# Seven block products for eight in the down projection and the embedding's gate of a decoder trunk

## The chip, the cores and the metric

The kernel runs on one core of a Trainium2 chip. The metric is the device time of one execution in microseconds (us). The engines are TensorE (PE in the profile; its weight loads are PEld), VectorE (DVE), ScalarE (ACT), GpSimd (POOL) and SyncE (SP), which issues the loads of the weights. They run side by side and wait for each other on semaphores.

## The reference

Two layers over 256 tokens of width 2048, all in fp32. In each layer the stream h receives three additions:

```
h += Mixer(RMSNorm(h))                                  # latent attention in layer 0, gated delta rule in layer 1
gate, up = split(RMSNorm(h) @ w_gate_up)                # 2048 x (2 x 5632)
h += (silu(gate) * up) @ w_down                         # 5632 x 2048
h += RMSNorm(p[i] @ w_proj) * sigmoid(RMSNorm(h) @ w_gate)   # w_gate 2048 x 2048
```

The mixers, which the change does not touch beyond their buffers, have projections of the same kind.

## The kernel before

**Products.** A weight is loaded in tiles of 4 k-tiles by 512 columns (`wload`, line 99; a tile `raw`, 1 MB). `wsplit` (L104) makes of it a rounded part `wh` (a cast on ScalarE, L109) and the remainder `wl` (a subtraction on VectorE, L110). The activations are split likewise, into `xh` and `xl`, after TensorE has transposed them (`make_xT`, L146). One product of a k-tile is then three matmuls of 512 columns, `xh wh`, `xh wl`, `xl wh` (`products`, L312 to L316). The 256 tokens are two row halves, t = 0 and 1. `linear` (L294) takes one block of 512 columns at a time: two banks of PSUM, one for each t, and for each k-tile two products, six matmuls. When a block is done its `evac` reads the banks.

**Seven for eight.** In the gate/up projection `seven` (L318) takes a gate block (columns c1) and an up block (c2) together. The first 8 of the 16 k-tiles form a 2 by 2 block matrix on both sides: A11 to A22 are the two token halves by the two groups of four k-tiles, b11 to b22 the two groups by the two blocks. Instead of eight block products it makes seven, of sums of blocks: A11 b11, S1 (b12 - b11), A12 b21, S2, S4 b22, S3, and A22. The sums of weight blocks are built on VectorE (L346, L356, L363, L372), those of activations once per norm (`Norm.operands`, L206). Four banks A, C, B, D take the results; two are copied in between by ScalarE (B from A, L351; m5, L353; u2, L360), and D begins as an addition on VectorE (L367). A call of one product over the four k-tiles is a `phase`: 12 matmuls. The other 8 k-tiles follow in the plain form, in phases of 12 as well.

**Stages.** `ffn` (L620) works in four parts of 3, 3, 3 and 2 middle blocks of 512: the part's gate/up calls, then the down projection of these blocks into all of h, with `linear`. Ahead of the last down projection `embed` (L649) makes the embedding's projection. `ple` (L682) is the gate, with `linear`. As soon as a block of h is complete, `Norm.block` (L258) makes the next stage's operands of it.

**What sets the order.** Each engine runs its instructions in one fixed order. The framework that builds the program fixes it: it takes the instructions in the order of the text as long as, by its own estimate, what they need is ready, and otherwise lets later ones pass. `tick` (L270) and `later` (L276) put small work (transposes of a finished block) between matmuls, a set number of ticks later.

**Buffers.** `raw`, `wh` and `wl` have three buffers each in a pool of the whole kernel (`WBUFS`, L40), and in `ffn` two, one and one more (`EXTRA`, L41; `wtile`, L90), so four for split weights there and three elsewhere. `S4` (L39) is the number of shared tiles of 128 x 1024, `P2` (L47) that of the 128 x 512 tiles of each stage. PSUM has four banks for products and four for transposes.

## Time and profile before

| | us |
|---|---|
| median of 3 runs (2805.26 to 2807.74) | 2806.23 |
| the profiled execution, its own time | 2807.84 |
| its span, first to last instruction | 2805.8 |
| PE matmuls busy (99%) | 2774.5 |
| VectorE busy (69%) | 1946.2 |
| ScalarE busy (51%) | 1443.5 |

A matmul's record is longer than its share of the engine, since matmuls are pipelined: the distance from one to the next is the cost. In lists by group, the number behind the last bar is the time that the engine sat idle just before such instructions, and what ended it. The gate/up and down projections of layer 0 run from about 297 to 1021 us, the embedding's projection inside it from 959 to 970, the gate from 1021 to 1089; layer 1 has the same stages from about 1990 to the end.

### The profile page before, as it was taken

The page shows a single profiled execution, that of the slowest core. Times are in us where ns is not written, and L with a number is a line of the kernel's source. Part 1 is how long each engine was busy: PE and PEld are TensorE (multiplying, and loading weights), DVE is VectorE, ACT ScalarE, POOL GpSimd, SP SyncE. Part 2 cuts the span into 40 slices and gives each one's busy share as a digit, 9 for nine tenths or more (in the row PEclk, how much of TensorE's full clock was granted, in tenths as well). Part 3 has the DMA queues.
Part 4 walks back from the last instruction along what each step waited for, and adds up shares of the span by engine and source line. Part 5 has one row for each costly group of instructions (what it writes and reads, how often), then busy time and mean ns, then how long its engine had stood idle before and what let it go on. Part 6 is the DMA issues. An engine that isn't in the chain of part 4 may idle for free.

```text
span 2805.8 us, 33510 instructions
## 1 busy us (share of the span) xinstructions
PE 2774.5 (99%) x13609; PEld 2300.1 (82%) x13609; DVE 1946.2 (69%) x1818; ACT 1443.5 (51%) x1517; POOL 161.6 (6%) x254
## 2 busy tenths in 40 slices
PE   8999999999999999999999999999999999999999
PEld 8778888888888888788888888888788888888887
DVE  5675876877867765556774556657985876867764
ACT  6765653654544555645444444444663554554553
POOL 1430000000000000222100000000000000000000
PEclk9999999999999999999999999999999999999999
DMA  7435465565565545666777545546555464655554
GB/s 225 128 115 190 165 246 174 210 210 171 189 225 195 196 154 175 210 223 213 268 247 237 189 150 188 174 159 215 180 207 198 173 232 150 240 195 194 183 171 145
DMA packets 296444, 540.81 MB, mean 193 GB/s; under 512 B 34105, under 2 KB 55266, under 8 KB 296034
## 3 DMA queue, kind: packets, MB, share of 16 engines
q1 hardware_dynamic: 295858, 536.58, 56.4%
q8 instruction: 107, 1.75, 0.3%
q10 hardware_dynamic: 432, 2.10, 0.2%
q14 instruction: 47, 0.39, 0.0%
HBM read 517.63 MB, written 21.00 MB: 192 GB/s over the span
## 4 chain that ended last, share of the span: by engine, by line
PE 50%; DVE 1%; ACT 1%; issue 1%; DMA 0%; POOL 0%; DVEq 0%; ACTq 0%
PE mm L314 15%; PE mm L316 15%; PE mm L315 15%; PE tr L965 1%; PE tr L1074 1%; PE tr L1080 1%; PE tr L155 1%; DVE wl L110 1%; ACT wh L109 0%; DMA raw<-in_ffn_w_gate_up 0%; PE tr L808 0%; PE tr L868 0%; PE tr L1055 0%; DVE vb L1133 0%; POOL r8o L122 0%
## 5 line engine op out<-in xcount | busy, mean ns | idle before, releaser
L110 DVE TENSOR_TENSOR wl<-raw,wh 128x2048 fp32r<-128x2048 f32 (+4 forms) x514 | 1120.7, 2191 | 546.6 <-ACT wh L109 545.6
L314 PE MATMUL mm<-wh,xh 128*128 128x512 f32 (+1 forms) x3600 | 1414.1, 393 | 5.2 <-ACT wh L109 5.1
L316 PE MATMUL mm<-wh,xl 128*128 128x512 f32 (+1 forms) x3600 | 1395.3, 388 | 0.0
L315 PE MATMUL mm<-wl,xh 128*128 128x512 f32 (+1 forms) x3600 | 1392.1, 387 | 0.9 <-DVE wl L110 0.9
L109 ACT CAST wh<-raw 128x2048 fp32r<-128x2048 f32 (+4 forms) x514 | 936.3, 1826 | 741.3 <-PE mm L316 588.6
L314 PEld LDWEIGHTS mm<-wh,xh 128*128 128x128 f32 x3600 | 678.4, 189 | 141.4 <-ACT wh L109 6.7
L316 PEld LDWEIGHTS mm<-wh,xl 128*128 128x128 f32 x3600 | 677.5, 188 | 138.1 <-DVE xl L593 0.2
L315 PEld LDWEIGHTS mm<-wl,xh 128*128 128x128 f32 x3600 | 678.8, 189 | 131.5 <-DVE wl L110 2.2
L109 ACT CAST wh<-tm 128x2048 fp32r<-128x2048 f32 x44 | 84.0, 1909 | 135.9 <-PE mm L316 115.0
L110 DVE TENSOR_TENSOR wl<-tm,wh 128x2048 fp32r<-128x2048 f32 x44 | 100.6, 2286 | 28.7 <-ACT wh L109 28.6
L400 DVE TENSOR_TENSOR h<-h,mm 128x512 f32<-128x512 f32 x104 | 68.8, 682 | 25.0 <-PE mm L316 24.9
L122 POOL TENSOR_TENSOR re<-re,neghalf 128x2 f32<-128x2 f32 x2 | 5.4, 2704 | 1348.0 <-DVE re L672 1348.0
L631 ACT ACTIVATE sg<-mm,rs 128x512 f32<-128x512 f32 x44 | 30.3, 689 | 62.1 <-PE mm L316 62.1
L346 DVE TENSOR_TENSOR tm<-raw 128x2048 f32<-128x2048 f32 x22 | 50.3, 2288 | 14.0 <-DMA raw<-in_ffn_w_gate_up 14.0
L363 DVE TENSOR_TENSOR raw<-raw 128x2048 f32<-128x2048 f32 x22 | 50.3, 2284 | 1.0 <-DMA raw<-in_ffn_w_gate_up 1.0
L356 DVE TENSOR_TENSOR tm<-raw,tm 128x2048 f32<-128x2048 f32 x22 | 50.4, 2292 | 0.7
L372 DVE TENSOR_TENSOR raw<-raw,tm 128x2048 f32<-128x2048 f32 x22 | 50.3, 2285 | 0.2
L164 ACT ACTIVATE xh<-tr,ncol 128x256 fp32r<-128x256 f32 x88 | 38.9, 476 | 22.2 <-PE tr L155 16.0
L816 DVE SCALAR_TENSOR_TENSOR vT<-tr,cw,vT 128x255 f32<-128x255 f32 (+2 forms) x96 | 40.1, 473 | 10.8 <-ACT vT L393 10.6
L165 DVE SCALAR_TENSOR_TENSOR xl<-tr,ncol,xh 128x256 fp32r<-128x256 f32 x88 | 39.4, 479 | 11.6 <-ACT xh L164 10.7
L177 ACT ACTIVATE junk<-h 128x512 f32<-128x512 f32 x48 | 29.9, 626 | 12.9 <-DVE h L400 10.1
L314 PE MATMUL mm<-wh,x 128*128 128x512 f32 x88 | 34.5, 392 | 0.0
(289 smaller groups left out, 1694.1 us busy)
## 6 DMA issues: line engine op xcount, KB each, us to landing
raw<-in_ffn_w_gate_up SPq DMA_DIRECT2D x176, 1024.0 KB, 5.7
raw<-in_gdn_w_in SPq DMA_DIRECT2D x92, 1024.0 KB, 5.3
raw<-in_ffn_w_down SPq DMA_DIRECT2D x88, 1024.0 KB, 5.2
raw<-in_ple_w_gate SPq DMA_DIRECT2D x32, 1024.0 KB, 5.0
raw<-in_gdn_w_out SPq DMA_DIRECT2D x32, 1024.0 KB, 5.2
raw<-in_mla_w_o SPq DMA_DIRECT2D x16, 1024.0 KB, 5.1
raw<-in_mla_w_ukv SPq DMA_DIRECT2D x8, 1024.0 KB, 5.4
raw<-in_mla_w_in SPq DMA_DIRECT2D x8, 768.0 KB, 4.9
```

The source lines that it names most:

```text
L109: nc.scalar.copy(out=wh[:, k:e, :n], in_=src[:, k:e, :n])
L110: nc.vector.tensor_sub(out=wl[:, k:e, :n], in0=src[:, k:e, :n], in1=wh[:, k:e, :n].bitcast(F32))
L165: nc.vector.scalar_tensor_tensor(out=xl[:, s], in0=ps[:, c:c + n], scalar=w, in1=xh[:, s].bitcast(F32), op0=ALU.mult, op1=ALU.subtract)
L314: mm(ps[:, :n], lhsT=xh, rhs=wh[:, kk, :n], start=start, stop=False, **kw)
L315: mm(ps[:, :n], lhsT=xh, rhs=wl[:, kk, :n], start=False, stop=False, **kw)
L316: mm(ps[:, :n], lhsT=xl, rhs=wh[:, kk, :n], start=False, stop=stop, **kw)
L346: nc.vector.tensor_sub(out=tm, in0=b12, in1=b11)
L356: nc.vector.tensor_sub(out=tm, in0=b22, in1=tm)
L363: nc.vector.tensor_sub(out=b12, in0=b22, in1=b12)
L372: nc.vector.tensor_sub(out=b21, in0=b21, in1=tm)
L400: nc.vector.tensor_add(out=h[bi][:, t, :], in0=h[bi][:, t, :], in1=ps[t])
L816: nc.vector.scalar_tensor_tensor(out=acc[:, o + s:o + 256], in0=src[:, 0:256 - s], scalar=cw[:, jj * 64 + f:jj * 64 + f + 1], in1=acc[:, o ...
```

## The change

`seven` is now also used by the down projection and the embedding's gate, in a form with s = 2: the 2 by 2 block matrix covers four k-tiles, two in each group, and the remaining k-tiles (8 or 4 in the down projection, 12 in the gate) follow in the plain form. A fast phase is then 6 matmuls and its split 2 k-tiles (128 x 1024). One call covers two blocks of 512 columns, so each down projection and each gate is two calls, and both blocks of a call end together. `Half` makes the operands for it: the two split parts of the whole 512 columns, and four sums S1 to S4 of 128 x 256 each, split as one. It stands in for `make_xT` for the first middle block of each part and for the first block of the gate's norm.

The subtractions of weight blocks are now in place, in both forms: b12 becomes b12 - b11, then b22 - b12; b11 becomes b12 - b11; b21 becomes b21 - b12. The tile `tm` is gone, and m5 and u2 come from the stage's pool of 128 x 512 tiles. With s = 2 the four blocks lie in two raw tiles, r1 (b11, b21) and r2 (b12, b22).

`EXTRA` buffers now also exist in the gate's stage. `S4` goes from 20 to 22; `P2` from 14 to 13 in the first mixer, from 1 to 2 in `ffn`, from 6 to 2 in `ple`.

```diff
@@ -36,15 +36,15 @@
 MLAG = 2
 Y1 = 4
 Y2 = 3
-S4 = 20
+S4 = 22
 WBUFS = {"raw": 3, "wh": 3, "wl": 3}
 EXTRA = {"raw": 2, "wh": 1, "wl": 1}
-NV0 = 1
 OGY = 5
 PRE = 1
 SY = 2
 KY = 3
-P2 = {"mla": 14, "gdn": 8, "ffn": 1, "ple": 6}
+NV0 = 1
+P2 = {"mla": 13, "gdn": 8, "ffn": 2, "ple": 2}
...
@@ -184,8 +184,8 @@
     class Norm:
-        def __init__(self, wcol, sums=False):
-            self.wcol, self.x, self.of7 = wcol, [], sums
+        def __init__(self, wcol, form=None):
+            self.wcol, self.x, self.form, self.half = wcol, [], form, None
             self.ss = sm(8, "ss")
         def sums(self, b):
@@ -198,8 +198,11 @@
                 rsqrt_(self.rs, 2)
         def parts(self, b):
-            if self.of7 and b < 2:
+            if self.form == 4 and b < 2:
                 self.operands(b)
+            elif self.form == 2 and b == 0:
+                self.half = Half(lambda t: h[b][:, t, :], gain(self.wcol))
+                self.x.append(self.half.x)
             else:
                 self.x.append(make_xT(lambda t: h[b][:, t, :], gain(self.wcol + 4 * b)))
...
-        def seven(self, name, kk):
+        def op(self, name, kk):
+            if self.form == 2:
+                until(lambda: self.half is not None)
+                return self.half.op(name, kk)
...
-    def seven(nrm, W, c1, c2, evac):
...
+    def seven(xs, op, s, W, kt, c1, c2, evac, row0=0, u2col=None):
         def bank():
             return psmm.tile([P, 512], F32, tag="mm", name="mm")
+        def phase(ps, x2, w2, n, start=False):
+            for kk in range(n):
+                products(ps, x2(kk), w2[0], w2[1], kk, 512, start and kk == 0, kk == n - 1, skip_group_check=True)
                 if kk % 2:
                     tick()
+        def fast(name):
+            return lambda kk: op(name, kk)
+        def std(k0, t):
+            return lambda kk: part(xs, k0 + kk, t)
+        if s == 4:
+            b11, b12 = wload(W, row0, c1), wload(W, row0, c2)
+            b21, b22 = wload(W, row0 + 512, c1), wload(W, row0 + 512, c2)
+        else:
+            r1, r2 = wload(W, row0, c1), wload(W, row0, c2)
+            b11, b21, b12, b22 = r1[:, 0:2], r1[:, 2:4], r2[:, 0:2], r2[:, 2:4]
+        A, C, B = bank(), bank(), bank()
+        phase(A, fast("A11"), wsplit(b11, s), s, True)
+        nc.vector.tensor_sub(out=b12, in0=b12, in1=b11)
+        w2 = wsplit(b12, s)
+        phase(C, fast("S1"), w2, s, True)
         nc.scalar.copy(out=B, in_=A)
+        m5, u2 = p2(name="m5"), p2(name="u2")
         nc.scalar.copy(out=m5, in_=C)
+        phase(B, fast("A12"), wsplit(b21, s), s)
         nc.vector.tensor_sub(out=b12, in0=b22, in1=b12)
+        phase(A, fast("S2"), wsplit(b12, s), s)
+        if u2col is None:
+            nc.scalar.copy(out=u2, in_=A)
+        else:
+            scaled(u2, A, u2col)
+        phase(C, fast("S4"), wsplit(b22, s), s)
+        nc.vector.tensor_sub(out=b11, in0=b12, in1=b11)
+        phase(A, fast("S3"), wsplit(b11, s), s)
         D = bank()
         nc.vector.tensor_add(out=D, in0=A, in1=m5)
+        for k in range(2 * s, kt, 4):
+            first, last = k == 2 * s, k + 4 >= kt
+            q1 = wsplit(wload(W, row0 + k * P, c1))
+            raw2 = wload(W, row0 + k * P, c2)
+            until(lambda: len(xs) > k // 4)
+            if first:
+                phase(B, std(k, 0), q1, 4)
+                nc.vector.tensor_sub(out=b21, in0=b21, in1=b12)
+                phase(A, fast("A22"), wsplit(b21, s), s)
+            q2 = wsplit(raw2)
+            phase(A, std(k, 1), q1, 4)
+            if last:
+                evac(0, 1, A, None)
+            if not first:
+                phase(B, std(k, 0), q1, 4)
+            if last:
+                evac(0, 0, B, None)
+            phase(C, std(k, 0), q2, 4)
+            if last:
+                evac(1, 0, C, u2)
+            phase(D, std(k, 1), q2, 4)
+            if last:
+                evac(1, 1, D, None)
+    class Half:
+        def __init__(self, src, gains):
+            xf = p4("xf")
+            for pair in range(2):
+                ps = trp()
+                for k2 in range(2):
+                    for t in range(T):
+                        kk = pair * 2 + k2
+                        nc.tensor.transpose(out=ps[:, k2 * 256 + t * P:k2 * 256 + (t + 1) * P],
+                                            in_=src(t)[:, kk * P:(kk + 1) * P], identity=ident)
+                if gains is None:
+                    nc.scalar.copy(out=xf[:, pair * 512:(pair + 1) * 512], in_=ps)
+                else:
+                    for k2 in range(2):
+                        kk = pair * 2 + k2
+                        scaled(xf[:, kk * 256:(kk + 1) * 256], ps[:, k2 * 256:(k2 + 1) * 256], gains[kk])
+            self.sums(xf)
+        def sums(self, xf):
+            self.x = xpair()
+            f = p4("f").rearrange("p (z k c) -> p z k c", z=4, k=2)
+            x4 = xf.rearrange("p (k t c) -> p k t c", k=4, t=T)
+            a11, a21, a12, a22 = x4[:, 0:2, 0, :], x4[:, 0:2, 1, :], x4[:, 2:4, 0, :], x4[:, 2:4, 1, :]
+            self.cut(*self.x, xf)
+            nc.vector.tensor_add(out=f[:, 0], in0=a21, in1=a22)
+            nc.vector.tensor_sub(out=f[:, 1], in0=f[:, 0], in1=a11)
+            nc.vector.tensor_sub(out=f[:, 2], in0=a11, in1=a21)
+            nc.vector.tensor_sub(out=f[:, 3], in0=a12, in1=f[:, 1])
+            s2 = xpair()
+            self.cut(*s2, f.rearrange("p z k c -> p (z k c)"))
+            self.s = [z.rearrange("p (z k c) -> p z k c", z=4, k=2) for z in s2]
+        @staticmethod
+        def cut(dh, dl, src):
+            nc.scalar.copy(out=dh, in_=src)
+            nc.vector.tensor_sub(out=dl, in0=src, in1=dh.bitcast(F32))
+        def op(self, name, kk):
+            if name[0] == "A":
+                return part([self.x], kk + (0 if name == "A11" else 2), int(name == "A22"))
+            return tuple(z[:, int(name[1]) - 1, kk] for z in self.s)
+    def of_half(hold):
+        def op(name, kk):
+            until(lambda: hold() is not None)
+            return hold().op(name, kk)
+        return op
...
+    def residual2(b0, nxt):
+        def evac(c, t, ps, u2):
+            z = h[b0 + c][:, t, :]
+            if u2 is not None:
+                nc.vector.tensor_add(out=z, in0=z, in1=u2)
+            nc.vector.tensor_add(out=z, in0=z, in1=ps)
+            if nxt is not None and (c, t) in ((0, 0), (1, 1)):
+                nxt.block(b0 + c, NLAG)
         return evac
@@ -622,6 +684,16 @@
         parts = [range(0, 3), range(3, 6), range(6, 9), range(9, NFF)]
         for pi, js in enumerate(parts):
             mid = []
+            def mids(mid, md):
+                if mid:
+                    mid.append(make_xT(lambda t: md[:, t, :], None))
+                else:
+                    hd = Half(lambda t: md[:, t, :], None)
+                    mid.append(hd.x)
+                    halves.append(hd)
+            halves = []
             for jb in js:
                 sg = p4("sg").rearrange("p (t n) -> p t n", t=T)
                 md = p4("md").rearrange("p (t n) -> p t n", t=T)
@@ -636,12 +708,14 @@
                     nc.vector.scalar_tensor_tensor(out=md[:, t, :], in0=ps, scalar=nrm.rs[:, t:t + 1],
                                                    in1=sg[:, t, :], op0=ALU.mult, op1=ALU.mult)
                     if t == T - 1:
-                        later(MLAG, lambda: mid.append(make_xT(lambda t: md[:, t, :], None)))
-                seven(nrm, wgu, jb * 512, FF + jb * 512, evac_gu)
+                        later(MLAG, lambda: mids(mid, md))
+                seven(nrm.x, nrm.op, 4, wgu, 16, jb * 512, FF + jb * 512, evac_gu)
             if pi == len(parts) - 1 and ahead is not None:
                 ahead()
-            linear(mid, wd, 4 * len(js), BLK, residual(nxt if pi == len(parts) - 1 else None), row0=js[0] * 512)
+            for b0 in (0, 2):
+                seven(mid, of_half(lambda: halves[0] if halves else None), 2, wd, 4 * len(js), b0 * 512, b0 * 512 + 512,
+                      residual2(b0, nxt if pi == len(parts) - 1 else None), row0=js[0] * 512)
...
-        def evac(bi, c0, n, ps):
...
+        def evac2(b0):
+            sgs = [p4("psg").rearrange("p (t n) -> p t n", t=T) for _ in range(2)]
+            def evac(c, t, ps, u2):
+                bi, sg = b0 + c, sgs[c]
+                if u2 is not None:
+                    nc.vector.tensor_add(out=sg[:, t, :], in0=ps, in1=u2)
+                    ps = sg[:, t, :]
+                nc.scalar.activation(out=sg[:, t, :], in_=ps, func=AF.Sigmoid, scale=nrm.rs[:, t:t + 1])
                 nc.vector.tensor_mul(out=sg[:, t, :], in0=sg[:, t, :], in1=es[bi][:, t, :])
                 nc.vector.tensor_add(out=h[bi][:, t, :], in0=h[bi][:, t, :], in1=sg[:, t, :])
+                if (c, t) not in ((0, 0), (1, 1)):
+                    return
+                if nxt is not None:
+                    nxt.block(bi, NLAG)
+                if last:
+                    nc.sync.dma_start(out=outv[:, :, bi * 512:(bi + 1) * 512], in_=h[bi])
+            return evac
+        for b0 in (0, 2):
+            seven(nrm.x, nrm.op, 2, a["ple_w_gate"][i], 16, b0 * 512, b0 * 512 + 512, evac2(b0))
...
@@ -1173,11 +1256,11 @@
             nrm.block(b)
     for n, (s, i) in enumerate(steps):
         last = n == len(steps) - 1
-        nxt = None if last else Norm(WC[kind[steps[n + 1][0]], steps[n + 1][1]], sums=steps[n + 1][0] == "ffn")
+        nxt = None if last else Norm(WC[kind[steps[n + 1][0]], steps[n + 1][1]], {"ffn": 4, "ple": 2}.get(steps[n + 1][0]))
         with ExitStack() as ctx:
             mc = ctx.enter_context(tc.tile_pool(name=f"{s}{n}", bufs=1))
-            scope["extra"] = mc if s == "ffn" else None
-            if s in ("mla", "ple"):
+            scope["extra"] = mc if s in ("ffn", "ple") else None
+            if s != "gdn":
                 scope["p2"] = ctx.enter_context(tc.tile_pool(name=f"{s}p2{n}", bufs=P2[s]))
             if s == "mla":
                 mla(i // 2, nrm, nxt, mc)
```

## Rows read from the trace of the kernel before

**Rows 1.** The page's head and part 1: busy us (share of the span) xinstructions.

```profile
span 2805.8 us, 33510 instructions
PE 2774.5 (99%) x13609; PEld 2300.1 (82%) x13609; DVE 1946.2 (69%) x1818; ACT 1443.5 (51%) x1517; POOL 161.6 (6%) x254
```

**Rows 2.** The page's part 5: busy us, mean ns, idle before, its end.

```profile
L314 PE MATMUL mm<-wh,xh 128*128 128x512 f32 (+1 forms) x3600 | 1414.1, 393 | 5.2 <-ACT wh L109 5.1
L315 PE MATMUL mm<-wl,xh 128*128 128x512 f32 (+1 forms) x3600 | 1392.1, 387 | 0.9 <-DVE wl L110 0.9
```

**Rows 3.** A window inside a down projection: PE busy (x), clock, DMA.

```profile
433.00:489.00 56.00, 56.00 (x247) 1.00 0.52 172
```

**Rows 4.** Windows by stage: busy PE, PEld, DVE, ACT, POOL, clock, DMA, GB/s.

```profile
440.00:491.00 51.00, 51.00 (x225) 41.98 (x224) 32.86 (x20) 17.19 (x9) 0.00 (x0) 1.00 0.50 165
532.00:574.00 42.00, 42.00 (x190) 34.65 (x189) 37.41 (x22) 24.71 (x18) 0.00 (x0) 1.00 0.56 200
962.30:1037.00 74.70, 74.70 (x346) 61.92 (x345) 54.41 (x61) 44.94 (x64) 5.76 (x6) 1.00 0.52 173
```

**Rows 5.** The chain that ended last, at its end: start, us, what.

```profile
2799.46 1.37 DVE psg L691 x2
2800.83 0.60 DVE h L692
```

**Rows 6.** Groups by line and shape, whole span: busy us, mean ns, idle before.

```profile
L110 DVE TENSOR_TENSOR wl<-raw,wh 128x2048 fp32r<-128x2048 f32 x466 | 1064.7, 2295 | 493.1 <-ACT wh L109 492.2
L109 ACT CAST wh<-raw 128x2048 fp32r<-128x2048 f32 x466 | 888.7, 1909 | 696.9 <-PE mm L316 546.8 <-DVE h L400 46.3 <-DMA raw<-in_ffn_w_gate_up 42.7
L400 DVE TENSOR_TENSOR h<-h,mm 128x512 f32<-128x512 f32 x104 | 68.8, 682 | 25.0 <-PE mm L316 24.9
L110 DVE TENSOR_TENSOR wl<-raw,wh 128x1024 fp32r<-128x1024 f32 x12 | 14.7, 1224 | 29.3 <-ACT wh L109 29.3
L109 ACT CAST wh<-raw 128x1024 fp32r<-128x1024 f32 x12 | 12.5, 1046 | 26.2 <-PE mm L316 26.2
L678 DVE SCALAR_TENSOR_TENSOR e<-e,re,pw 128x512 f32<-128x512 f32 x16 | 11.0, 745 | 1.4 <-POOL re L122 1.2 <-DMA pw<-in_ple_norm 0.2
L667 DVE COPY e<-mm 128x512 f32<-128x512 f32 x16 | 10.6, 683 | 4.5 <-PE mm L316 4.5
```

**Rows 7.** Timeline of VectorE, gate/up calls: start, us, instruction, idle before.

```profile
496.45 2.29 DVE L110 TENSOR_TENSOR wl<-raw,wh 128x2048 fp32r<-128x2048 f32 x1 [0.68 <-ACT wh L109]
499.17 4.62 DVE L110 TENSOR_TENSOR wl<-raw,wh 128x2048 fp32r<-128x2048 f32 x2 [0.43 <-ACT wh L109]
581.26 6.68 DVE L110 TENSOR_TENSOR wl<-raw,wh 128x2048 fp32r<-128x2048 f32 x3
```

**Rows 8.** Timeline of ScalarE in a gate/up call.

```profile
494.02 0.57 ACT L351 COPY mm<-mm 128x512 f32<-128x512 f32 x1 [0.77 <-PE mm L316]
496.74 0.59 ACT L353 COPY m<-mm 128x512 f32<-128x512 f32 x1 [0.33 <-PE mm L316]
499.55 1.91 ACT L109 CAST wh<-raw 128x2048 fp32r<-128x2048 f32 x1 [0.41 <-ACT wh L109]
502.28 0.59 ACT L360 COPY u<-mm 128x512 f32<-128x512 f32 x1 [0.81 <-PE mm L316]
```

**Rows 9.** Timeline at the start of a gate/up call: the first matmul of A11.

```profile
491.10 0.39 PE L314 MATMUL mm<-wh,x 128*128 128x512 f32 x1
```

**Rows 10.** Groups of VectorE, 225 to 300 us, making operands.

```profile
L225 DVE TENSOR_TENSOR xl<-f,xh 128x1024 fp32r<-128x1024 f32 x2 | 2.4, 1214 | 0.0
L165 DVE SCALAR_TENSOR_TENSOR xl<-tr,ncol,xh 128x256 fp32r<-128x256 f32 x4 | 1.7, 476 | 0.0
```

**Rows 11.** Groups from 962.3 to 1021.6 us: transposes of blocks of h.

```profile
L155 PE MATMUL tr<-ident,h 128*128 128x128 f32 x31 | 4.0, 272 | 0.0
```

**Rows 12.** Loads of the gate/up weight, from issue to landing, us.

```profile
DMA to landing us min/median/max: 4.8/5.7/10.0
```

**Rows 13.** A window at the kernel's start, columns as in rows 4.

```profile
8.00:13.00 5.00, 1.94 (x7) 1.81 (x8) 3.35 (x13) 3.27 (x6) 0.00 (x0) 1.00 1.02 358
```

More of the change, by code (lines that the diff above doesn't have):

```diff
@@ L221, in operands @@
             x4 = xf.rearrange("p (k t c) -> p k t c", k=4, t=T)
-            def split(dh, dl, src):
-                nc.scalar.copy(out=dh, in_=src)
-                nc.vector.tensor_sub(out=dl, in0=src, in1=dh.bitcast(F32))
+            split = Half.cut
             if b == 0:
@@ L330, in phase @@
                 if kk % 2:
                     tick()
-        def op(name):
-            return lambda kk: nrm.seven(name, kk)
-        def std(q, t):
-            return lambda kk: part(nrm.x, 4 * q + kk, t)
-        b11, b12 = wload(W, 0, c1), wload(W, 0, c2)
-        b21, b22 = wload(W, 512, c1), wload(W, 512, c2)
-        cs = scope["extra"]
-        w2 = wsplit(b11)
-        A = bank()
-        phase(A, op("A11"), w2, True)
-        tm = cs.tile([P, 4, 512], F32, tag="tm", name="tm", bufs=1)
@@ L346, in seven @@
-        nc.vector.tensor_sub(out=tm, in0=b12, in1=b11)
-        w2 = wsplit(tm)
-        C = bank()
-        phase(C, op("S1"), w2, True)
-        B = bank()
+        def fast(name):
[8 more added lines that the diff above has]
+            b11, b21, b12, b22 = r1[:, 0:2], r1[:, 2:4], r2[:, 0:2], r2[:, 2:4]
```

49 lines of the change are left out of this document (1 added, 48 removed).

## The prediction

> **What bounds the kernel now.** I read the page's head and busy times first: TensorE's matmuls are busy 2774.5 of 2805.8 us, and VectorE, the next engine, 1946.2 [rows 1]. A pipelined engine can look busy and still stall, so next come the groups of matmuls with the idle time ahead of them: in the three product lines TensorE waited 5.2 us for a ScalarE cast and 0.9 us for a VectorE remainder in the whole run [rows 2]. Then its pace: 247 matmuls touch a stretch of 56.00 us in the down projection, about 246 whole pitches, so 0.2276 us each at a granted clock of 1.00 [rows 3]. The kernel is bound by the number of matmuls, nearly everywhere. What matters next is how near the second engine is. Windows by stage [rows 4]: in a gate/up call VectorE works 37.41 of 42 us, in the down projection 32.86 of 51, from the embedding's projection into the gate 54.41 of 74.7. In both of the last two the change moves work onto VectorE.
>
> I sum against the profiled execution's own 2807.84 us (span 2805.8 and 2 us around it); the median of the runs shown is 2806.23, so 1.6 is taken off at the end.
>
> **What it removes.** For two column blocks and four k-tiles the plain form takes 2 x 4 x 2 x 3 = 48 matmuls, seven products of two k-tiles take 7 x 2 x 3 = 42. The down projection makes 4 parts x 2 calls x 2 layers = 16 such calls, the embedding's gate 2 x 2 = 4. So 20 x 6 = 120 matmuls go, all on the path: 120 x 0.2276 = 27.3 us. [...]
>
> At the very end the last block's two halves no longer finish together: now two multiplications and two additions stand in the chain after the last matmul [rows 5], afterwards one of each. About 0.6 each: 1.2 us.
>
> **What it adds, and where.** Durations are from the groups by shape [rows 6]; back to back, three remainders of 2048 columns take 6.68 us, so one costs 2.2 [rows 7], and I take 0.09 off the others likewise: 1.14 for 1024 columns, 0.60 for 512. A call's two full splits (4.4 on VectorE) become seven half splits and four half subtractions, 11 x 1.14 = 12.5, with one addition into bank D and one of u2 (1.2): 9.3 us more per call, 186 in all. Over the whole span this fits easily. So the stages decide, and in them three places.
>
> *Place 1, the short phases of every call.* A product is now 6 matmuls, 1.37 us, where the gate/up's is 12, 2.73. Four buffers hold split weights. The first full split of a call (q1) takes over the third product's buffer, free 3 x 1.37 = 4.10 after the call begins, and TensorE wants q1 after six products, at 8.19, its remainder one matmul later, 8.42. Between: 0.2 until ScalarE sees a product's end (the copy at 494.02 comes so after A11's [rows 8, 9]), cast 1.91, remainder 2.29 [rows 6]: 8.5. That is 0.1 late with both engines free. They are not: on ScalarE the copy m5 (0.59) and the cast for S3 stand ahead of it until about 4.6, so q1's cast ends at 6.4 and its remainder at 8.7; and behind this cast waits the copy u2, wanted at 5.66, done at 7.0, and TensorE may not write bank A for S3 (due at 6.83) before. Together 0.3 to 0.6; I take 0.5. Below: 0, if the framework's order finds TensorE other products meanwhile. Above: u2 placed ahead of q1's cast; then copy until 6.25, cast until 8.1, remainder until 10.4, 2.0 late. In the gate/up the same chain has 8.2 us instead of 4.1, so rows 2 show nothing of it. Sixteen calls are of this kind (the other four are in place 2): 8 us, bounds 0 and 32. [...]
>
> *Place 2, the last part of each layer.* It has two k-groups only: a call is 90 matmuls, 20.5 us, and VectorE's share is 12.5 + 4.4 + 0.6 + five additions of 0.60 [rows 6] = 20.5. No slack, and it lies between the embedding's projection and the next norm. From 962.3 (inside that projection) until the gate's A22 product I add up VectorE: the projection's eight copies and eight scalings (0.60, 0.66 [rows 6]), two halves of the last middle block and the small ones, 11.6; two calls, 41.0; operands of block 0, two of 1.14 and four of about 0.40 [rows 10], 3.9; block 1, four of these, 1.6; then the gate's opening, 12.5 + 4.4 + 0.6, and blocks 2 and 3, 3.2: 78.7, of which one subtraction is done earlier, 77.6. TensorE has 8.0 + 41.0 + 15.0 and 32 transposes of 0.13 [rows 11], 68.2. VectorE is 9.4 us short, where it had 20 to spare [rows 4]. The scalings (5.3) are not urgent, but come first in the program and have run as soon as they could; if they wait, 4.1 are short. Some lead of finished weights covers part of it. Bounds 0 and 10; I take 6, towards the sum: 12 us for two layers. What is late is A12, S2 and S3 of both calls.
>
> *Place 3, the gate/up itself.* Its subtractions are now all in place, so b11's buffer is kept until the S3 split instead of the first subtraction, and the weights of the second full group load later. In the call that begins at 491.1 [rows 9] the S3 remainder runs from 499.17 for 2.29 [rows 7] and ends 10.4 after the start; load 5.7 [rows 12], cast 1.91, remainder 2.29: 20.3, wanted after nine phases, at 24.6. Covered by 4 us; with the slowest landing (10.0 [rows 12]) by nothing. Bounds 0 and 4.2 (one full split) for 22 calls; I take 0. The middle block's new operands add 2.7 us to VectorE in one call of three. The remainders for S4, S3 and q1 are done at 498.7, 501.5 and 503.8 [rows 7] and due at 502.0, 504.8 and 507.5: 3.3 us of lead, 2.1 where a middle block's halves (1.2) come between. 0 to 0.6 for 8 calls; taken 0.
>
> The gate's larger rings start in memory of the stage before; all such openings, the kernel's start among them, lie within rows 2's waits: 0 to 2 us each, taken 0.5 each, 1. One buffer fewer in the first mixer: rows 2 leave no wait for it there; 0, at most one operation of 0.6 for each of 8 head pairs, 5; taken 0.
>
> Sum: -27.3 - 1.2 + 8 + 12 + 1 = -7.5: 2800.3 for a profiled execution, 2798.7 against the median, rounded 2799.
>
> **Rivals.**
> *The cover holds.* The gate/up already runs VectorE at 89% without a stall [rows 2, 4], and products can be ordered around a late one. Then places 1 and 2 cost 4 us together: -28.5 + 4 = -24.5, 2782. Against it: the chain of place 1 is longer than its cover even with idle engines.
> *Nothing comes of it.* Place 2 costs its full 9.5 a layer and place 1 0.5 a call: -28.5 + 19 + 8 + 1 = -0.5, 2806. For it: place 2's sum is work, which no order makes less.
> *Slower: u2 ahead of q1.* One mechanism, place 1's upper end: ScalarE's order puts the copy u2 before q1's cast. From 1.0 us a call on, with 12 in place 2, the gain is gone; at 2.0 it is -28.5 + 32 + 12 + 1 = +16.5, 2823. For it: u2 comes first in the program, and S3's product waits for it. Against: in the gate/up q1's cast, at 499.55, ran before u2, at 502.28 [rows 8].
> [...]
>
> **Chances.** Forecast 0.47, cover holds 0.16, nothing 0.15, slower 0.20, clock 0.02. This kernel can be told from no change by about 0.2%, 5.6 us. Faster takes the cover case and about three quarters of the forecast, 0.51; within 0.2% the rest of the forecast and nearly all of the third case, 0.26; slower 0.23. The likeliest case alone reaches from 2791 to 2803; with the others at both ends the range is 2782 to 2818.
>
> **What would show it.** Right: 3560 products with xh in each of the three lines where 3600 stand [rows 2], VectorE about 200 us busier; idle time ahead of the first and second product lines 10 to 30 us, ended by casts and remainders, some in every call of the down projection and most between the embedding's projection and the gate; none more in the gate/up; clock 1.00. Idle ahead of S3 ended by the copy u2 would show place 1 as worked out, idle of 2 us ahead of q1 its upper end. Wrong: under 5 us of idle (cover holds), idle in the gate/up ended by loads (place 3), or idle over 30.

## The result, and the profile after

The changed kernel takes 2838.65 us (median of 4 runs, 2834.11 to 2839.36), the kernel before 2806.51 beside it: ratio 1.0113, 95% interval 1.01 to 1.0125. It is 32 us slower; the forecast was 2799 and its range ended at 2818.

The head and busy times of the page after. They answer to [rows 1].

```profile
span 2837.6 us, 33807 instructions
PE 2774.4 (98%) x13489; PEld 2278.3 (80%) x13489; DVE 2153.1 (76%) x2074; ACT 1550.7 (55%) x1698; POOL 160.6 (6%) x254
```

The 120 matmuls are gone (13489 of 13609), VectorE has 207 us more. The two product groups that answer to [rows 2]:

```profile
L317 PE MATMUL mm<-wh,xh 128*128 128x512 f32 (+3 forms) x3560 | 1407.4, 396 | 29.3 <-ACT wh L109 26.9 <-ACT u L359 2.1
L318 PE MATMUL mm<-wl,xh 128*128 128x512 f32 (+3 forms) x3560 | 1384.5, 389 | 9.0 <-DVE wl L110 8.8
```

3560 products, as worked out, and 38 us of idle time where 6 stood: 26.9 of it ended by a cast on ScalarE, 8.8 by a remainder on VectorE. Where it is, the first matmuls of the stages tell (distances of their starts in the three traces, us; the last column is the best kernel found, E9 below):

| stretch | before | after | E9 |
|---|---|---|---|
| first gate/up call of layer 0 | 42.99 | 46.88 | 42.98 |
| first two gate/up calls of layer 1 | 87.34 | 90.55 | 85.54 |
| third call and down projection of the second part | 108.55 | 106.56 | 106.56 |
| embedding's projection to the recurrent stage, layer 0 | 165.66 | 186.32 | 165.78 |
| recurrent stage until the second feed-forward | 864.71 | 857.98 | 856.42 |
| embedding's projection to the end, layer 1 | 152.14 | 173.25 | 152.13 |

The six parts gain 2.0 us each (the first 1.2), and the opening gate/up calls lose 3.9 and 3.2. The stretches from the embedding on lose 20.7 and 21.1 although each has 24 matmuls, 5.5 us, fewer: 26 to 27 us lost a layer, about 20 and 21 of them up to the gate's first matmul (in layer 1, 4.4 of these in one wait at that matmul), 6 and 5 behind it. In the two stretches I add up what matmuls start later than 0.2276 us after their forerunner: 34.5 us where TensorE waited, and 12.6 where they follow each other at 0.427, at a granted clock of 0.50. The recurrent stage, which no edit touches, is 6.7 us shorter; the last section comes back to it.

Windows of after (engine order PE, PEld, DVE, ACT, POOL, then clock, DMA share and GB/s): a plain stretch, and four pieces of the last part of layer 0, which answer to [rows 4].

```profile
440.00:491.00 51.00, 51.00 (x223) 41.40 (x223) 44.31 (x33) 25.13 (x19) 0.00 (x0) 1.00 0.65 225
962.00:973.00 11.00, 11.00 (x50) 9.02 (x49) 10.78 (x16) 10.15 (x23) 0.43 (x1) 1.00 0.12 44
973.00:1000.00 27.00, 22.87 (x83) 16.64 (x82) 21.72 (x23) 11.79 (x18) 1.17 (x1) 0.81 0.48 175
1000.00:1022.00 22.00, 15.71 (x55) 11.01 (x54) 20.86 (x24) 16.29 (x21) 0.00 (x0) 0.85 0.14 49
1022.00:1038.00 16.00, 16.00 (x76) 13.07 (x75) 14.66 (x20) 9.38 (x19) 0.00 (x0) 1.00 0.57 196
```

Beside the projection both VectorE (10.78 of 11) and ScalarE (10.15) are full. After that TensorE stands (busy 22.87 of 27 and 15.71 of 22), and the mean granted clock is 0.81 and 0.85. The same place closer, in timelines of VectorE, ScalarE and TensorE (start, us, instruction, idle before):

```profile
974.21 2.74 DVE L752 SCALAR_TENSOR_TENSOR e<-e,re,pw 128x512 f32<-128x512 f32 x4 [0.59 <-POOL re L122]
976.86 1.22 DVE L110 TENSOR_TENSOR wl<-raw,wh 128x1024 fp32r<-128x1024 f32 x1
978.00 1.22 DVE L363 TENSOR_TENSOR raw<-raw 128x1024 f32<-128x1024 f32 x1
979.13 2.74 DVE L752 SCALAR_TENSOR_TENSOR e<-e,re,pw 128x512 f32<-128x512 f32 x4
981.78 3.60 DVE L110 TENSOR_TENSOR wl<-raw,wh 128x1024 fp32r<-128x1024 f32 x2
...
975.37 1.90 ACT L109 CAST wh<-raw 128x2048 fp32r<-128x2048 f32 x1 [1.59 <-PE mm L319]
979.25 1.05 ACT L109 CAST wh<-raw 128x1024 fp32r<-128x1024 f32 x1 [1.98 <-DVE raw L363]
980.68 0.58 ACT L359 COPY u<-mm 128x512 f32<-128x512 f32 x1 [0.38 <-PE mm L319]
981.16 1.90 ACT L109 CAST wh<-raw 128x2048 fp32r<-128x2048 f32 x1
...
977.32 0.51 PE L317 MATMUL mm<-wh,xh 128*128 128x512 f32 x1 [1.99 <-ACT wh L109]
...
981.31 0.79 PE L317 MATMUL mm<-wh,xh 128*128 128x512 f32 x1 [0.68 <-ACT u L359]
983.11 0.79 PE L317 MATMUL mm<-wh,xh 128*128 128x512 f32 x1 [1.01 <-ACT wh L109]
983.71 0.63 PE L318 MATMUL mm<-wl,xh 128*128 128x512 f32 x1
984.13 0.63 PE L319 MATMUL mm<-wh,xl 128*128 128x512 f32 x1
```

TensorE's first wait, 1.99 us, ends with the cast of the call's first full split (q1, at 975.37), which had itself waited 1.59 us for TensorE. VectorE keeps to its order: four scalings of the embedding (L752), begun at 974.21, run ahead of the remainder at 976.86, whose cast was done at 973.79, and of the difference L363 (978.00). ScalarE's cast waits 1.98 us for that; the copy u2 comes at 980.68, after 0.38 us of waiting for TensorE, the cast of the second full split (q2) at 981.16, and TensorE stands again; its next matmuls, as at 983.71 and 984.13, start 0.42 apart.

### The profile page after: what moved, and what is told of

Its sections match the earlier page's. It is cut to its first block, busy times and chain, and to the rows that moved or that the text cites. A ratio compares the mean times of both kernels' runs of the same rounds, so it can differ in the third digit from the quotient of the medians.

```text
span 2837.6 us, 33807 instructions
## 1 busy us (share of the span) xinstructions
PE 2774.4 (98%) x13489; PEld 2278.3 (80%) x13489; DVE 2153.1 (76%) x2074; ACT 1550.7 (55%) x1698; POOL 160.6 (6%) x254
## 4 chain that ended last, share of the span: by engine, by line
PE 46%; DVE 4%; ACT 1%; issue 1%; DMA 1%; POOL 0%; SPq 0%; DVEq 0%; ACTq 0%
PE mm L317 14%; PE mm L319 14%; PE mm L318 14%; DVE wl L110 2%; PE tr L1048 1%; ACT wh L109 1%; PE tr L1157 1%; PE tr L1163 1%; PE tr L155 0%; PE tr L891 0%; PE tr L951 0%; PE tr L1138 0%; DMA raw<-in_ffn_w_down 0%; DVE xl L428 0%; DVE xl L165 0%
## 5 line engine op out<-in xcount | busy, mean ns | idle before, releaser
L110 DVE TENSOR_TENSOR wl<-raw,wh 128x2048 fp32r<-128x2048 f32 (+3 forms) x658 | 1295.7, 1986 | 402.5 <-ACT wh L109 400.8
L109 ACT CAST wh<-raw 128x2048 fp32r<-128x2048 f32 (+3 forms) x658 | 1083.6, 1663 | 814.2 <-PE mm L319 588.7
L317 PE MATMUL mm<-wh,xh 128*128 128x512 f32 (+3 forms) x3560 | 1407.4, 396 | 29.3 <-ACT wh L109 26.9
L318 PE MATMUL mm<-wl,xh 128*128 128x512 f32 (+3 forms) x3560 | 1384.5, 389 | 9.0 <-DVE wl L110 8.8
L319 PE MATMUL mm<-wh,xl 128*128 128x512 f32 (+3 forms) x3560 | 1384.5, 389 | 0.0
L349 DVE TENSOR_TENSOR raw<-raw 128x2048 f32<-128x2048 f32 (+1 forms) x42 | 74.7, 1779 | 13.4 <-DMA raw<-in_ffn_w_down 10.2
L356 DVE TENSOR_TENSOR raw<-raw 128x2048 f32<-128x2048 f32 (+1 forms) x42 | 74.8, 1781 | 1.0
L363 DVE TENSOR_TENSOR raw<-raw 128x2048 f32<-128x2048 f32 (+1 forms) x42 | 74.8, 1781 | 0.8
L374 DVE TENSOR_TENSOR raw<-raw 128x2048 f32<-128x2048 f32 (+1 forms) x42 | 74.7, 1777 | 0.2
L462 DVE TENSOR_TENSOR h<-h,mm 128x512 f32<-128x512 f32 x64 | 43.6, 683 | 21.7 <-PE mm L319 21.1
L352 ACT COPY mm<-mm 128x512 f32<-128x512 f32 x42 | 24.1, 573 | 21.1 <-PE mm L319 21.1
L359 ACT COPY u<-mm 128x512 f32<-128x512 f32 x42 | 24.9, 593 | 17.6 <-PE mm L319 17.6
```

The lines of the kernel that those rows point to most:

```text
L109: nc.scalar.copy(out=wh[:, k:e, :n], in_=src[:, k:e, :n])
L110: nc.vector.tensor_sub(out=wl[:, k:e, :n], in0=src[:, k:e, :n], in1=wh[:, k:e, :n].bitcast(F32))
L317: mm(ps[:, :n], lhsT=xh, rhs=wh[:, kk, :n], start=start, stop=False, **kw)
L318: mm(ps[:, :n], lhsT=xh, rhs=wl[:, kk, :n], start=False, stop=False, **kw)
L319: mm(ps[:, :n], lhsT=xl, rhs=wh[:, kk, :n], start=False, stop=stop, **kw)
L349: nc.vector.tensor_sub(out=b12, in0=b12, in1=b11)
```

## The experiments

**Which products lose.** Four kernels take parts of the change back.

E1: the last part of each down projection plain.

```diff
+            if pi == len(parts) - 1:
+                linear(mid, wd, 4 * len(js), BLK, residual(nxt), row0=js[0] * 512)
+                continue
             for b0 in (0, 2):
                 seven(mid, ...)
```

> The last part of each layer's down projection (8 k-tiles, beside the embedding's projection) is again eight products for eight; the other three parts and the gate keep seven. Theory A: the loss of the changed kernel is made in that last part, where VectorE has too much to do (20.7 and 21.1 us of the trace in the two stretches from the embedding to the next layer's start or the end). Then those stretches fall to some 164 us and the time to 2791 to 2798. Rival B: the loss is made by the gate (half operands that are late, its short phases); then at most a quarter of it goes: 2826 to 2838. Rival C: the loss is the in-place subtraction in the gate/up calls and the buffers traded for it; then nearly nothing goes: 2834 to 2842.

2813.33 (2810.9 to 2817.4). 25 us come back, fewer than the 41 to 48 of theory A and more than B or C allow: the last part is the largest loss, not the only one.

E2: the gate plain.

```diff
-        for b0 in (0, 2):
-            seven(nrm.x, nrm.op, 2, a["ple_w_gate"][i], 16, b0 * 512, b0 * 512 + 512, evac2(b0))
+        linear(nrm.x, a["ple_w_gate"][i], 16, BLK, evac)
```

> The embedding's gate is again eight for eight with its operands as before; the whole down projection keeps seven. Theory A (last part of the down projection): the stretches keep their loss, the gate's gain of about 1 us a call goes: 2838 to 2844. Rival B (the gate): 2791 to 2800. Rival C (gate/up calls and buffers): 2836 to 2842.

2832.99, under the ranges of A and C and above B's: beside a last part with seven the gate costs 5.7.

E3: both edits.

> Seven products only in the first three parts of each down projection; last part and gate as before the change; rings, in-place subtractions and 22 large buffers as after. Theories A and B: 6 parts x -2.0 us, the recurrent stage -6.7, the gate/up calls +7: 2793 to 2798, under the kernel before by 8 to 13. Rival C: above the kernel before, 2815 to 2840.

2797.69, ratio to before 0.9972 (0.9963 to 0.9981). Against E1 the gate alone loses 15.6, for 24 matmuls saved.

E4: E2's edit, and all four parts plain; buffers and in-place form stay.

```diff
-            for b0 in (0, 2):
-                seven(mid, ...)
+            linear(mid, wd, 4 * len(js), BLK, residual(nxt if pi == len(parts) - 1 else None), row0=js[0] * 512)
```

> No seven products in the down projection or the gate at all; what is left of the change is the buffers (22 large ones, rings in the embedding's stage, 13 and 2 small ones) and the in-place subtractions and order of issue in the gate/up calls. Theories A and B: recurrent stage -6.7, gate/up calls +7, so 2803 to 2809, the kernel before. Rival C: 2825 or more. If the recurrent stage's gain is not the buffers', 2810 to 2815.

2811.15, ratio 1.0026 (1.0016 to 1.0035), the last of the three cases: 5.7 us slower than the kernel before with no product changed. So the three parts gain 13.5 (E4 to E3), and the buffers and the in-place form, which I had taken at nothing, cost.

**The in-place differences.** E9 is built on the kernel before: its gate/up form with `tm`, 20 large buffers, the gate as it was; the new `seven` is there as `seven2`.

```diff
+            if pi == len(parts) - 1:
+                linear(mid, wd, 4 * len(js), BLK, residual(nxt), row0=js[0] * 512)
+                continue
+            for b0 in (0, 2):
+                seven2(mid, of_half(...), 2, wd, 4 * len(js), b0 * 512, b0 * 512 + 512, residual2(b0, ...), row0=js[0] * 512)
```

> The kernel before with its own gate/up form (the tile tm, 20 large buffers, the gate's rings as before), and seven products only in the first three parts of each down projection. Theory A: 6 parts x -2.0 us = -12 and none of the 5.7 that buffers and in-place form cost: 2790 to 2794 where the kernel before takes 2805. Rival: the 5.7 come from something else that the new operands need anyway (the half operands in the opening gate/up calls): 2796 to 2800.

2787.30 (2785.68 to 2793.55), ratio 0.9945 (0.9932 to 0.9958): 17 us faster than the kernel before, and 3 under theory A's range. Of the 21.2 us between the two traces the parts give 12 and the recurrent stage, which this edit does not touch either, 8.3.

E10: E9 with one edit.

```diff
-        nc.vector.tensor_sub(out=tm, in0=b12, in1=b11)
-        w2 = wsplit(tm)
+        nc.vector.tensor_sub(out=b12, in0=b12, in1=b11)
+        w2 = wsplit(b12)
...
-        nc.vector.tensor_sub(out=b12, in0=b22, in1=b12)
-        w2 = wsplit(b12)
+        nc.vector.tensor_sub(out=b11, in0=b12, in1=b11)
+        w2 = wsplit(b11)
...
```

> The kernel of the run before it with one edit: the gate/up's weight differences are made in place, without tm, as in the changed kernel. If the in-place form is what cost 5.7 us (b11 and b12 kept longer, so loads of the next weights start later while the opening calls have no lead), 5 to 7 us slower than the kernel with tm, with the loss in the first two gate/up calls of each layer; if 22 large buffers or the order of the evacuations are, 0 to 1.

2800.57 (2796.53 to 2803.41): 13.3 slower. In the traces 5.3 and 5.0 lie between the first gate/up call and the second part of the two layers, 4.8 in the recurrent stage. The last 4.8 are not the edit's: E10's trace has 20.5 us at a granted clock of 0.50 there, E9's 10.2, and half the difference, which I estimate as lost by that clock, is 5.1. So the in-place form costs about 10 in the gate/up. The reason given in the expectation is not what the timelines show. First VectorE in E9's first gate/up call, then VectorE, ScalarE and TensorE in E10's:

```profile
303.01 2.29 DVE L372 TENSOR_TENSOR raw<-raw,tm 128x2048 f32<-128x2048 f32 x1
```

```profile
308.23 6.68 DVE L110 TENSOR_TENSOR wl<-raw,wh 128x2048 fp32r<-128x2048 f32 x3
314.83 2.28 DVE L371 TENSOR_TENSOR raw<-raw 128x2048 f32<-128x2048 f32 x1
...
317.21 1.90 ACT L109 CAST wh<-raw 128x2048 fp32r<-128x2048 f32 x1 [6.19 <-DVE raw L371]
...
319.16 0.50 PE L314 MATMUL mm<-wh,xh 128*128 128x512 f32 x1 [0.43 <-ACT wh L109]
321.23 0.73 PE L314 MATMUL mm<-wh,xh 128*128 128x512 f32 x2 [1.57 <-ACT wh L109]
```

With `tm` the framework puts A22's difference (b21 minus S2's matrix) ahead of these remainders (L372, at 303.01), in place behind them (L371, at 314.83). ScalarE waits 6.19 us for it, and the casts of the next products come behind, from 319.28.

E5 and E6 write that difference earlier, in the changed kernel and in E3.

```diff
+        nc.vector.tensor_sub(out=b21, in0=b21, in1=b12)
         nc.vector.tensor_sub(out=b11, in0=b12, in1=b11)
```

> The changed kernel, with the difference for A22 (b21 - b12) written directly after S2's, ahead of S3's, where it was written only after the first plain phase. No work is added or taken away. Theory D: what the changed kernel loses is lost by VectorE's order, above all this difference, for which ScalarE's cast and everything queued behind it wait; then the opening gate/up calls get back 3 us a layer and the stretch from the embedding to the gate 5 to 10 a layer: 2812 to 2825. Rival E: it is the amount of VectorE's work in that stretch, and no order helps: 2834 to 2843, or 2832 if the opening gate/up calls alone gain.

2837.96, no change, as rival E gave.

> Seven products in the first three parts alone (last part and gate plain), again with the A22 difference early. Theory D: the 5.7 us that the buffers and the in-place form cost without any new products (2811.2 against 2805.5) are this difference, late in the opening gate/up calls of each layer: 2790 to 2793 against 2797.7 of the same kernel with it late. Rival: they are the raw buffers held longer: 2796 to 2800.

2801.99 (2797.84 to 2806.32), above both ranges and 4 slower than E3. The first two calls of layer 1 fall from 90.5 to 86.4, but the second call of layer 0 rises from 42.1 to 48.0, where the middle block's half operands now come in: earlier in the text is not a cure, the loss only moves.

**The gate's rings.** In E1, SyncE, ScalarE and TensorE at the opening of layer 1's gate:

```profile
2706.10 0.92 SPq L101 DMA_DIRECT2D raw<-in_ple_w_gate  x2
...
2711.24 1.04 ACT L109 CAST wh<-raw 128x1024 fp32r<-128x1024 f32 x1 [1.85 <-DMA raw<-in_ple_w_gate]
...
2712.34 0.80 PE L317 MATMUL mm<-wh,xh 128*128 128x512 f32 x1 [4.62 <-ACT wh L109]
```

The gate's loads go out only at 2706.10, among the last residual additions of the stage before, and TensorE stands 4.62 us. E12 keeps one pool for both stages of a layer.

```diff
+        if s == "ffn":
+            rings = ExitStack()
+            scope["extra"] = rings.enter_context(tc.tile_pool(name=f"rings{n}", bufs=1))
...
-            scope["extra"] = mc if s in ("ffn", "ple") else None
...
```

> The changed kernel with the extra ring buffers kept in one pool from the feed-forward stage through the gate, instead of a new pool for the gate that takes over memory of the stage before. In the kernel with a plain last part TensorE stood 4.66 us at the gate's opening of layer 1, its loads issued only when the last residual was added, and the clock was low for 6.8 us after. If the new pool is what holds the gate's first loads: 4 to 9 us less, 2829 to 2835. If these loads are hidden behind VectorE's lateness in the changed kernel: 2836 to 2841.

2830.10: 8.5 less, in the first range. In the stretch to the end of layer 1 the stalls fall from 18.1 to 12.2 us.

**The last part: work, order or lead.** E7 issues the scalings inside the gate.

```diff
...
+            for b in (b0, b0 + 1):
+                later(9 if b == b0 else 2, lambda b=b: gains(b))
             seven(nrm.x, nrm.op, 2, a["ple_w_gate"]...
```

> The changed kernel, with the eight multiplications that scale the embedding's projection (0.66 us each on VectorE) issued inside the gate instead of ahead of the last part's down projection; the same work later. Theory E (amount of work in the stretch, about 26 us lost a layer where VectorE is some 10 short): 5.3 us of work leave the worst place, so at least 5 a layer come back, up to 10 with the clock that falls in the stalls: 2818 to 2829. Rival: the work only moves into the gate, which is itself short (15.6 us were lost by the gate alone): 2834 to 2843.

2827.14, 11.5 less, 6.8 and 5.0 in the two stretches: as expected of theory E. E8, this and E5's edit together:

> Both edits of order in one kernel. If order is what costs, the sum of both: 2800 to 2815, with the granted clock above 0.994 in the stretches from the embedding to the gate. If the amount of work is, no better than the better one alone.

2832.79: 5.7 slower than E7 alone; the two do not add up.

E11 moves `ahead()` ahead of the last part's gate/up calls.

> The changed kernel with the embedding's projection and its scalings moved ahead of the last part's gate/up calls, so about 10 us of VectorE's work a layer leave the stretch between the last gate/up call and the gate. Theory E (amount of work: VectorE some 10 us short there, and stalls, low clock and lost lead on top): 15 us a layer or more come back, 2805 to 2822. Rival: order alone, other places are late instead: 2830 to 2845.

2839.95, the rival. From the last gate/up call to the gate 14 and 9 us come back, but the gate/up call behind the projection takes 51.6 and 51.5 us instead of 41.1, and the part before it 2 more than the projection's 11: the loss goes where the projection goes.

E13 takes about 10 us a layer off VectorE.

```diff
-                nc.vector.tensor_copy(out=es[bi][:, t, :], in_=ps[t])
+                nc.scalar.copy(out=es[bi][:, t, :], in_=ps[t])
...
-                nc.vector.scalar_tensor_tensor(out=es[b][:, t, :], ...
```

> The changed kernel with about 10 us of VectorE's work a layer left out or taken off it beside the last part: the scalings of the embedding's projection are left out of the computation, its eight copies are made by ScalarE. Theory E (VectorE's work there is what is short; moved elsewhere, as in the run with the embedding earlier, it is short there): 12 to 20 us a layer come back, 2800 to 2815. Rival (the short phases and ScalarE's order lose the time, whatever VectorE has to do): 2828 to 2840, the more so as ScalarE has 5 us more.

2829.95: 8.7 less, in the rival's range and outside theory E's 2800 to 2815. E18 takes the work off both engines, by leaving out `square_sum` and scalings, and the copies of blocks 1 to 3.

```diff
+            if bi:
+                nc.gpsimd.memset(es[bi], 0.5)
+                return
```

> The changed kernel with nearly all elementwise work of the embedding's projection left out of the computation (copies of three of its four blocks, all squares, the scalings): about 9 us a layer off VectorE and 6.5 off ScalarE, the matmuls stay. Rival G (time of ScalarE and VectorE together is what is short; the run with the copies on ScalarE only moved the load): the stalls of the last part fall under 4 us a layer: 2800 to 2815. Theory F (lead): 8 to 10 come back as there: 2826 to 2832.

2816.61: 22 back, 1.6 short of G's range. Some 30 of the 53 us of the two stretches stay (they take 173.8 and 163.2 us). Windows beside the projection and after it, first of E13, then of E18:

```profile
962.00:973.00 11.00, 9.29 (x39) 6.87 (x37) 3.41 (x4) 10.90 (x28) 0.00 (x0) 1.00 0.11 42
973.00:1000.00 27.00, 22.98 (x100) 17.76 (x100) 23.51 (x24) 17.18 (x24) 1.60 (x1) 1.00 0.44 155
```

```profile
962.00:973.00 11.00, 11.00 (x50) 9.05 (x49) 10.57 (x10) 6.32 (x9) 0.00 (x0) 1.00 0.06 22
973.00:1000.00 27.00, 25.55 (x118) 20.09 (x116) 23.46 (x25) 18.57 (x29) 0.00 (x0) 1.00 0.46 156
```

In E13 VectorE has 3.41 us to do and ScalarE 10.90 of 11: the full engine has only changed. In E18 ScalarE is free again (6.32 of 11), VectorE (10.57) works ahead for the coming products, and TensorE makes 118 matmuls in the next 27 us where after made 83. The first product line from the last gate/up call to the gate of layer 0, in after, E13 and E18:

```profile
L317 PE MATMUL mm<-wh,xh 128*128 128x512 f32 x118 | 49.6, 421 | 8.5 <-ACT wh L109 7.8 <-ACT u L359 0.7
```

```profile
L317 PE MATMUL mm<-wh,xh 128*128 128x512 f32 x118 | 47.6, 405 | 6.3 <-ACT wh L109 2.7 <-ACT xh L164 1.5 <-ACT u L359 0.9
```

```profile
L317 PE MATMUL mm<-wh,xh 128*128 128x512 f32 x118 | 47.6, 405 | 4.1 <-ACT wh L109 1.7 <-ACT xh L164 1.5 <-ACT mm L352 0.8
```

E14: E9 with seven products in the last part too, and the projection behind it.

```diff
-            if pi == len(parts) - 1 and ahead is not None:
-                ahead()
```

> The best kernel so far (three parts, 2787.3) with seven products in the last part too, and the embedding's projection moved out of it, behind the last part into the gate's stage, whose products are plain. Theory E: without the projection beside it VectorE has 20.5 us of work in a call of 20.5; stalls of 0 to 5 us a layer between the last gate/up call and the gate, where 12.4 and 11.7 stood with the projection there. Rival: 10 or more stay, since calls of only two k-groups are too short by themselves.

2802.83, 15.5 more than E9; but the stalls of the last part are as theory E gave. Its first product line from the last gate/up call to the projection:

```profile
L314 PE MATMUL mm<-wh,xh 128*128 128x512 f32 x116 | 46.0, 400 | 1.1 <-ACT u L431 0.7 <-ACT wh L109 0.4
```

1.1 us idle instead of 8.5 (1.7 in layer 1). Seven gains nothing there all the same: from the last gate/up call to the last residual addition it is 90.1 and 91.3 us, in E9, plain, 90.4 and 90.5 without the projection's 11.1. The time is lost at the projection, which now opens the gate's stage and waits for its input (3.76 us of idle ahead of its first transpose in layer 0).

E16 puts two consecutive half splits into one buffer; E17 does so in E9.

```diff
+        if pair:
+            z = [t[:, 2:4] for t in pair]
+            pair.clear()
+        else:
+            pair.extend((wtile("wh", F32R), wtile("wl", F32R)))
+            z = [t[:, 0:2] for t in pair]
```

> The changed kernel with two consecutive half splits in one buffer of the rings wh and wl (A11 with S1, A12 with S2, S4 with S3), where each half split took a whole buffer of 4 k-tiles. No work and no memory is added; four buffers now hold up to eight fast products' weights, 11 us of TensorE's time, where they held four, 5.5 us. Theory F: the loss beside the projection and in the gate is lead: casts and remainders can't run ahead, since the buffers are full of halves. Then most of the stalls of the two stretches go (34.5 us of stalls and 12.6 of low clock): 2795 to 2815. Rival G: what is short there is the time of ScalarE and VectorE themselves: 2830 to 2840. If the write of the second half waits for the readers of the first, slower than 2840.

2824.61: 14 back, between the theories. Stalls in the two stretches 25.7 instead of 34.5, low clock 6.0 instead of 12.6. Lead is a part of the loss, not most.

> The best kernel so far (seven products in three parts, 2787.3) with two half splits in one buffer. Theory F, and the chain of place 1 (the first plain split takes a buffer that the third product frees): the 0.37 us that a call still loses go in part, 0 to 4.4 in all: 2783 to 2787. If shared buffers make new waits: 2788 to 2800.

2787.01 (2783.92 to 2788.72), the same as E9; ratio to before 0.9932 (0.9917 to 0.9947). In the traces the six parts take 3.2 us less than in E9 (105.97 against 106.56 in the second of layer 0), as the chain of place 1 would have it; the first two calls of layer 1 take 1.8 more and the recurrent stage 2.8 more.

E15: the changed kernel with `tm` and 20 large buffers, E12's pool and E7's scalings.

> The changed kernel with three things mended at once: the tile tm again in the gate/up (and 20 large buffers), the rings kept from the feed-forward stage into the gate, the embedding's scalings inside the gate; all products as in the changed kernel. If the causes found are separate, the sum of what each gave alone: 2838.7 - 13.3 - 8.5 - 11.5 = 2805. If they are one shortage that shows in several places: 2812 to 2825.

2811.57 (2808.49 to 2815.83), just under the range of one shortage: 27 of the 33 that the three gave one by one, and still 24 above E9, which has plain products in the last part and the gate.

## Why the prediction was wrong

**Removed: right.** 120 matmuls, 27.3 us. Of the tail's 1.2, 0.5 came: from the last matmul's end to VectorE's last addition 2.65 us before, 2.17 after. Its end, which answers to [rows 5]:

```profile
2832.42 0.70 DVE psg L770
2833.12 0.02 issue
2833.14 0.69 DVE h L771
```

One multiplication and one addition went, as worked out. But before, the first half's sigmoid on ScalarE had begun at 2798.74, ahead of the last matmul's end at 2799.38, so a part of the four was not behind it:

```profile
2798.74 1.37 ACT L690 ACTIVATE psg<-mm,rs 128x512 f32<-128x512 f32 x2 [13.73 <-PE mm L316]
```

**Place 1: right in the first three parts.** A part of two calls gains 2.0 of 2.73, so a call loses 0.37; I took 0.5. In the first call of the second part S3's first matmul starts right behind the end of the copy u2, 0.33 after its forerunner instead of 0.23, as worked out (ScalarE, then TensorE):

```profile
626.23 0.62 ACT L359 COPY u<-mm 128x512 f32<-128x512 f32 x1
...
626.57 0.40 PE L319 MATMUL mm<-wh,xl 128*128 128x512 f32 x1
626.90 0.51 PE L317 MATMUL mm<-wh,xh 128*128 128x512 f32 x1
```

E17, which eases this chain's buffers, gives 0.27 a call back. The copy u2 ends only 2.1 us of idle time in the whole run, and q1's cast at 975.37 runs ahead of it (980.68): the slower rival, u2 ahead of q1, did not come. That u2 would wait on ScalarE behind q1's cast, a part of the 0.5, was my estimate; no run shows that wait by itself. They show 0.37 a call in all, and in the call above u2 at 626.23, without idle time behind two casts of xh (625.28, 1.08 us). For the gate's four calls, of the same sixteen, 0.5 was too little (see place 2).

**Place 2: the step that failed.** The term was "I take 6 ... 12 us for two layers", bounds 0 and 10 a layer. It measured 20 and 21 up to the gate's first matmul, 26 to 27 with the gate; the 4.4 at that matmul in layer 1 belong to the ring openings. The place, and VectorE's work there, were right; three things were missing from the sum. ScalarE was not in it: with its casts, squares and copies it is full beside the projection too (10.15 of 11), and each half split needs one engine after the other (the cast 1.05, then the remainder 1.22). E18 shows that the embedding's elementwise work on both engines makes 22 of the loss, E14 that the stalls of the short products nearly go without it (1.1 idle); E13 shows that VectorE's sum alone does not decide. Next, the deficit of one engine is not the stall of another: a half split fills a whole buffer, so no lead builds up (E16, 14 back), and in two orders VectorE and TensorE wait for each other in turns, which is read from the timelines and was not tested by itself. And at a granted clock of 0.50 many matmuls took 0.427 us each instead of 0.2276 (12.6 us more). The gate belongs here as well: its calls had the 0.5 of place 1, its opening a share of place 2's sum. Against a plain last part it is 15.6 slower in all (E1 to E3); E12's pool, tried in the changed kernel, gave 8.5 back.

**Place 3: taken 0, measured 7.1** in the opening calls of the changed kernel against the one before, about 10 in E10 against E9. I had looked at loads in the steady calls, where indeed nothing waits. The loss is in the opening calls, where VectorE also makes the norm's operands and the framework's order leaves A22's difference for last. "Wrong: idle in the gate/up ended by loads" stood among the signs; the idle came, ended by casts. "Idle over 30" stood there too, and 38 came.

**Ring openings: taken 1, measured 8.5** (E12), at one of two gates, layer 1's; they are counted in the 27 of that layer.

**The clock falls: given 0.02, and it happens**, only not over all of place 2. The window at the kernel's start has 1.00 [rows 13]; later the trace of before has 0.50 too. Windows of before in the recurrent stage, and of after in place 2 (two of layer 0, two of layer 1, then the ends of the waits in which these last two began):

```profile
1155.00:1165.60 10.60, 8.29 (x37) 6.54 (x35) 6.92 (x8) 6.46 (x7) 5.15 (x3) 1.00 0.34 112
1165.60:1175.80 10.20, 9.17 (x30) 7.92 (x31) 2.37 (x2) 2.76 (x2) 5.14 (x4) 0.50 0.86 265
```

```profile
978.00:988.00 10.00, 8.18 (x18) 5.59 (x19) 9.22 (x11) 3.44 (x4) 0.00 (x0) 0.50 0.20 63
1015.50:1022.00 6.50, 5.89 (x14) 4.61 (x15) 5.71 (x5) 4.35 (x4) 0.00 (x0) 0.50 0.45 161
2691.50:2698.00 6.50, 6.13 (x14) 4.84 (x15) 6.46 (x6) 2.85 (x2) 0.00 (x0) 0.50 0.77 271
2739.00:2746.00 7.00, 4.92 (x11) 3.55 (x12) 6.45 (x6) 4.20 (x5) 0.00 (x0) 0.51 0.36 136
...
2691.87 0.80 PE L318 MATMUL mm<-wl,xh 128*128 128x512 f32 x1 [4.03 <-DVE wl L110]
2740.55 0.79 PE L317 MATMUL mm<-wh,xh 128*128 128x512 f32 x1 [4.39 <-ACT wh L109]
```

At 0.50 the starts of matmuls of 512 columns lie 0.427 us apart, at 1.00 0.2276 [rows 3]. In layer 1 the clock fell inside waits of 4.03 and 4.39 us, in layer 0 where TensorE waited 1 to 2 us at a time; the traces show the waits and the falls together, and no run tests whether the one brings the other.

Left open: how the 41 us of last part and gate divide exactly between work, lead and order, since these overlap (E15) and some 30 us stay without the embedding's elementwise work (E18), and why the framework places A22's difference last in the in-place form.

## What to carry to other kernels

Before a product is halved, count for each engine that feeds it, not only the fullest, the work per product in the stage where other work lies beside it, and the buffers that one product now fills; use the faster form only where a stage keeps a surplus on all of them (here three parts of four: 17 us gained instead of 32 lost, 14 of the 17 at the same clock). An edit that saves memory, in place instead of into a tile of its own, can change the order in which the framework issues, and has to be timed by itself. Price a stall at more than its length where the granted clock falls with it: here 34.5 us of stalls came with 12.6 more from matmuls at 0.50.

## What the runs showed of the hardware

In after, where TensorE is 98% busy, stretches of 3.4 to 10.2 us at a granted clock of 0.50 came behind waits of 1 to 2 us and, two of 6.8 us in layer 1, began inside waits of 4.0 and 4.4 us. Matmuls of 512 columns then lie 0.427 us apart instead of 0.2276. The recurrent stage, which no edit touches, has such stretches too, with a wait of 3.3 us that ended at 1166.6, and not the same ones in every run: 27.2 us of them in the trace of before, 13.7 in after's, 10.2 in E9's. Half the difference of before and E9, my estimate of what the clock of 0.50 costs, is 8.5 us, and the stage takes 864.71 and 856.42 in the two: 8.3; after's 857.98 fits likewise. The kernel before repeats within 2800 to 2809, and its times go with the granted clocks: of the 17 beside E9, the six with a mean of 0.998 took 2800.0 to 2800.6 us, the five with 0.995 took 2807.1 to 2808.6, and 0.003 of 2805 us is 8.4. At 0.998 E9 took 2785.7 to 2786.3, so its gain at the same clock is 14 us. Why the clock falls in one run and not in the next is not shown.
